# Two-layer decoder step: gained weights of the next layer formed behind a wait on the down products, last factors written in the down stage, two norm factors asked for later

## The chip, the cores and the metric

One core of a Trainium2 chip runs the whole program. The metric is the device time in microseconds (us), the median of the runs. The engines are named as the profile names them: PE (matmul), PEld (the loading of PE's weights), DVE (vector engine), ACT (scalar engine), POOL (GpSimd), SP (which here only issues transfers). A row such as `L246` is line 246 of the kernel before.

## The reference

Two layers run over 1024 prompt tokens and 8 decode tokens, width 1024, MLP width 4096. The parts that matter here are the MLP, which ends each layer, and the two projections that begin layer 1: the shared keys and values (`w_kv`, behind the gain `norm_kv`) and the queries (`w_in_b`, behind the gain `norm_mix_pre[1]`).

```python
def rmsnorm(x, g):
    xf = x.astype(jnp.float32)
    y = xf * lax.rsqrt(jnp.mean(xf * xf, axis=-1, keepdims=True) + EPS)
    return (y * g.astype(jnp.float32)).astype(x.dtype)

def squared_relu_mlp(h, w_up, w_down):
    return jnp.square(jax.nn.relu(h @ w_up)) @ w_down

for l in range(DEPTH):
    if l == N_A_LAYERS:
        ks, vs = jnp.split(rmsnorm(x, norm_kv) @ w_kv, 2, axis=-1)
    h = rmsnorm(x, norm_mix_pre[l])
    ...
    q, qm = split_cols(h @ w_in_b[bl], IN_B_SIZES)
    ...
    f = squared_relu_mlp(rmsnorm(x, norm_ffn_pre[l]), w_ffn_up[l], w_ffn_down[l])
    x = x + rmsnorm(f, norm_ffn_post[l])
```

## The kernel before

All matrices are float32. Each operand of a large matmul is cut into a high and a low part (`split`, L156 to L158: a cast on ACT, a subtraction on DVE), and each product is three matmuls (high by high, high by low, low by high).

**The MLP** (`mlp`) is the same code for both layers, with `l` the layer. Its **up stage** first does 4 of the 32 row tiles of `w_up` plainly (`up_plain`; the squared results go to the buffer `apd` in device memory), and then the other 28 as 14 pairs. A pair is one 2x2 block product done with seven products instead of eight: `wino_weights` (L660 to L675) makes the seven weight combinations on DVE from two loaded tiles `ws`, `product` (L838) runs a product, and `evict` (L640 to L653) adds each PSUM bank into the four results `c11` to `c22` on DVE, whose tile is named `aw` (`am` for the three combinations that `factors` makes). A pair is 168 matmuls of 258 columns. Its results go to the buffer `awd` in device memory. The four plain tiles need four such combinations too: `plain_factors` (L869) loads them from `apd` into tiles `c`, combines them on DVE (L878), and writes them to `awd` (L879). It is a generator: one step is taken at the fourth product of a pair from the sixth pair on.

The **down stage** is a loop of 64 phases (L1127). Phase `t` belongs to one of seven products and does 48 matmuls; the last 16 phases are half as wide. `load_w` fetches a weight block `wr` five phases ahead, `load_a` a factor block `ra` three phases ahead into two buffers (`rap`), `prep` (L984) cuts both two phases ahead, and `phase` (L1033) issues the matmuls; where a product ends, `gather` adds eight PSUM banks into `acc` on DVE. `kept["mm"]` is the name of the last matmul of the phase.

**The folds.** In layer 0 the loop also calls `fold` (L240) twelve times, once for each of the twelve weight tiles of layer 1's first projections. A fold is two halves, and each half is: POOL issues a load of 256 KB into a tile `t` (tag `t3`, two buffers), POOL multiplies it by the gain (128x512, L246), POOL issues the store to the buffer `wfd` in device memory (L247). SP loads from `wfd` at the end of the down stage and after it (L220). The table `folds` gives the phase that calls each fold: 2 to 6, 25 to 29, 36 and 38. A fold's load is placed behind `kept["mm"]` by a dependency of the kind `NOSYNC`.

**What sets the order.** A scheduler puts each engine's instructions in one list when the program is built; an engine runs its list strictly in order. A `NOSYNC` dependency orders two instructions for this scheduler alone and makes no engine wait at run time. A `SYNC` dependency puts a semaphore wait into the instruction. So before the change a fold's load waits only for its tile to be free.

**The norm factors.** `Closing` handles one of four pieces of the MLP's output (pa, pb, pc, pd). `feed` sums squares, `factor` turns them into the norm factor by a matmul with a matrix of ones (L204: `sf<-rb` for pc, `sx<-rf` for pd), two ACT and three DVE instructions. Its second argument says behind how many matmul columns the scheduler puts that matmul; `unit` is 9216 columns.

Of the kernel before, what the change touches and what calls it, by code (L numbers as in the profile page):

```python
# [8 lines left out]
F32 = mybir.dt.float32  # L9
# [7 lines left out]
P = 128  # L17
# [21 lines left out]
ORDER = (1, 7, 6, 5, 2, 3, 4)  # L39
# [10 lines left out]
def hybrid_decoder_step(ctx: ExitStack, tc: tile.TileContext, A, O):  # L50
# [14 lines left out]
    rp = ctx.enter_context(tc.tile_pool(name="rstd", bufs=1))  # L65
# [26 lines left out]
    def nm(s):  # L92
        uid[0] += 1
        return f"{s}_{uid[0]}"
# [2 lines left out]
    turn = [0, 0]  # L97
    xsp = [None]
    late = []
    NOSYNC = mybir.DependencyInfo(mybir.DependencyClass.NoSync, mybir.DependencyReason.DATA)  # L100

    class Row:
# [3 lines left out]
        def __call__(self, mm):  # L106
            if self.prev is not None:
                tc.add_manual_dep(mm.ins, self.prev, NOSYNC, reason="row of tiles")
            self.prev = mm.ins.name
# [16 lines left out]
    def tick(mm, cols):  # L126
        for it in list(late):
            it[1] -= cols
            if it[1] <= 0:
                late.remove(it)  # L130
                tc.add_manual_dep(it[0], mm.ins.name, NOSYNC, reason="behind later matmuls")

# [16 lines left out]
    def tmp3(shape):  # L149
        return view(tp.tile([P, 768], F32, tag="t3", name=nm("t3")), shape)  # L150
# [88 lines left out]
    def fold(i, behind):  # L239
        src, g = (A["w_kv"][i], G_KV) if i < 4 else (A["w_in_b"][i - 4], G_MIXPRE + 1)  # L240
        for h in range(2):
            ks = slice(4 * h, 4 * h + 4)
            ws = tmp3([P, 4, P])
            d = nc.gpsimd.dma_start(ws, src[:, ks, :])
            tc.add_manual_dep(d.ins, behind, NOSYNC, reason="behind later matmuls")
            nc.gpsimd.tensor_tensor(ws, ws, gains[:, g, ks].unsqueeze(2).to_broadcast([P, 4, P]), ALU.mult)  # L246
            nc.gpsimd.dma_start(wfd[i][:, ks, :], ws)  # L247

# [366 lines left out]
    class Slots:  # L615
# [3 lines left out]
        def next(self):  # L619
            self.half ^= 1  # L620
            if self.half == 0:
                self.cur = self.slots[self.i % len(self.slots)]
                self.i += 1
            ks = slice(4 * self.half, 4 * self.half + 4)
            return self.cur[0][:, ks, :], self.cur[1][:, ks, :]
# [50 lines left out]
    def mlp(l, X, ff):  # L676
# [192 lines left out]
        def plain_factors():  # L869
            for q in range(2):  # L870
                rows = [tp.tile([P, 768], F32, tag=tag, name=nm("c"))[:, :HALF] for tag in ("t3", "t3", "tq", "tq")]
                for r, (m, h) in zip(rows, ((0, 0), (0, 1), (1, 0), (1, 1))):
                    nc.sync.dma_start(r, apd[l, :, 2 * q + m, h, :])
                c11, c12, c21, c22 = rows
                for f_, r, a, b, op in ((1, c12, c22, c12, ALU.subtract), (4, c11, c12, c11, ALU.add),
                                        (6, c21, c11, c21, ALU.subtract), (5, c22, c22, c11, ALU.subtract)):
                    yield
                    TT(r, a, b, op)  # L878
                    nc.sync.dma_start(awd[l, f_, NJ - 1, :, q, :], r)  # L879

        plain = plain_factors()
        prepare(2)
        next(xsteps.pop(0))
        pend = None
        for t, (j, i) in enumerate(items):
            if i == ORDER[0]:
                if j == 0:
                    tiles = [tp.tile([P, 768], F32, tag=tag, name=nm("c")) for tag in ("t3", "t3", "tq", "tq")]
                    rows = [x[:, :HALF] for x in tiles]
                else:  # L890
                    tiles = [ff.pools[j % 2].tile([P, 4, HALF], F32, tag="f", name=nm("aw"))]
                    rows = [tiles[0][:, q] for q in range(4)]
            if xsteps:
                next(xsteps.pop(0))
                if xsteps:
                    next(xsteps.pop(0))
            prepare(t + (3 if j == 0 else 5))
            product(j, i, rows)
            if i == ORDER[0] and pend is not None:
                factors(*pend[2:])  # L900
                store(*pend)
                pend = None
            if i == ORDER[3] and 2 <= j < 5:
                square_mean(j - 2)
            if i == ORDER[3] and j >= 5:
                next(plain, None)
            if i == ORDER[-1]:
                more = w4.tile([P, 3, HALF], F32, tag="w4", name=nm("am"))
                pend = (j, tiles, rows, more)
# [75 lines left out]
        def prep(t):  # L985
            p, jj, s = phases[t]
            i = DOWN[p]
            r1, r2 = reg(1, jj), reg(2, jj) if p else None
            r3 = reg(3, jj) if p > 1 else None
            if i == 7:  # L990
                TT(r1, r1, r2, ALU.subtract)
            if i == 6:
                TT(r1, r3, r1, ALU.subtract)
            if i == 4:
                TT(r2, r2, r3, ALU.add)
            wh, wl = wsl[t % 3] if s is None else lasting(jj)
            if s is None or s == 0 and jj > 3:
                split(wh, wl, {1: r1, 7: r1, 6: r1, 5: r2}.get(i, r3))
            if i == 2:
                TT(r3, r3, r1, ALU.subtract)  # L1000
            raw = raws.pop(t)
            n = raw.shape[-1]
            sa = sas[t % 3]
            split(sa[:, 0, :, :n], sa[:, 1, :, :n], raw)
            ready[t] = (wh, wl, sa)
# [52 lines left out]
        unit = 3 * KT * 384  # L1058
        early, late_ = (acc[11], acc[21]), (acc[12], acc[22])
        rb = rbp.tile([P, SUB], F32, tag="rb", name=nm("rb"))  # L1060
# [8 lines left out]
        pc = piece(late_, slice(0, SUB), "sf", (1, 0, SUB))  # L1069
        pd = piece(late_, slice(SUB, HALF), "sx", (1, SUB, 384 - SUB), (2, 132, 132))  # L1070
# [13 lines left out]
        def hook(v):  # L1084
            if -8 <= v < -4:
                split(*lasting(v + 8), reg(3, v + 8))
            if v == -4:
                pa.feed(0, 1, 2, 3)
            if v == 0:
                rooms((pa, "xh0"), (pc, "xl0"))  # L1090
                pa.factor(rp.tile([P, 384], F32, tag="rf", name=nm("rf")), 0.3 * unit)
            if v == 1:
                pb.feed(0, 1, 2, 3)
                pb.factor(rx, 2 * unit)
            if v == 2:
                pa.close(behind=kept["mm"])
            if v == 4 and not l:
                hl[0] = xtiles(0)
                pa.cut(hl)
            if v == 5:  # L1100
                rooms((pb, "xl2"))
                pb.close(behind=kept["mm"])
            if v == 7:
                pc.feed(2, 3, 0, 1)
                pc.factor(rb, 1.8 * unit)
            if v == 9:
                pc.close((2, 3, 0, 1), behind=kept["mm"])
            if v == 11:
                rooms((pd, "xh2"))
            if v == 10 and not l:  # L1110
                rt[0] = rtile(0)
                pa.measure(0, rt[0], 2.3 * unit, Ring())
            if v == 11 and not l:
                hl[1] = xtiles(1)
                pc.cut(hl)
                hl[2] = xtiles(2)
                pb.cut(hl)
# [5 lines left out]
        with tc.high_priority(100):  # L1123
            prep(0)
            prep(1)
        folds = dict(zip((2, 3, 4, 5, 6, 25, 26, 27, 28, 29, 36, 38), (2, 3, 0, 1, 10, 11, 4, 5, 6, 7, 8, 9)))
        for t in range(N):  # L1127
            for u in ([3, 4, 5] if t == 0 else [t + 5]):
                if u < N:
                    load_w(u)  # L1130
            if t + 3 < N:
                load_a(t + 3)
            if t + 2 < N:
                with urgent(2) if t + 2 >= 6 * NJ else ExitStack():
                    prep(t + 2)
            phase(t)
            if l == 0 and t in folds:
                fold(folds.pop(t), kept["mm"])
            hook(t - 6 * NJ)

        st2.close()
        if l:
            with urgent(2):
                pd.finale()
                pd.factor(rp.tile([P, 384], F32, tag="rf", name=nm("rf"))[:, : pd.n], 0)
            pd.close()
        else:
            xs = pool(st, "right", "xs", 3)
            mq = pool(st, "right", "mq", 2)
            pd.feed(2, 3, 0, 1)  # L1150
            pd.factor(rp.tile([P, 384], F32, tag="rf", name=nm("rf"))[:, : pd.n], 1.3 * unit)
            pd.close((2, 3, 0, 1), xs)
            pd.cut(hl, (2, 3, 0, 1))
            rt[1] = rtile(1)
            pc.measure(1, rt[1], 4 * unit, mq)
            pd.measure(1, rt[1], 5 * unit, mq)
            rt[2] = rtile(2)
            pb.measure(2, rt[2], 9 * unit, mq)
            pd.measure(2, rt[2], 10 * unit, mq)
            res = [(hl[c], rt[c]) for c in range(3)]  # L1160
# [1052 lines left out]
```

## Time and profile before

| what | time |
|---|---|
| median of 3 runs (2213.41 to 2217.82) | 2216.09 us |
| the profiled execution, its own time | 2217.6 us |
| its span, first to last instruction | 2215.8 us |
| mean granted PE clock, share of full speed | 0.992 |
| layer 0: seven-product part of the up stage | 536.4 to 844.4 us |
| layer 0: down stage, first to last matmul | 844.4 to 1175 us |
| layer 1: seven-product part of the up stage | 1586.3 to 1872.6 us |
| layer 1: down stage | 1872.6 to 2201 us |
| POOL, all of it | 111.4 us busy |

In a profile row of the stretches, each engine's busy time stands with its number of instructions in brackets (x), then the granted clock, the mean busy share of the 16 DMA engines, and GB/s. In a timeline row the columns are start, duration, engine, line, operation, and in square brackets how long the engine had stood idle and what ended it. In a row of waits: who waited for whom, microseconds in total, how many times, the longest. In a row of a group: count, then busy us, mean ns of one, and idle time before it.

### The profile page before, as it was taken

How to read it: one execution, taken by the hardware profiler on the slowest of the kernel's cores; microseconds unless marked ns; L12 is line 12 of the kernel's file. 1: busy time of each engine (PE TensorE's matmuls, PEld its weight loads, DVE VectorE, ACT ScalarE, POOL GpSimd, SP SyncE). 2: the span in 40 equal slices, each digit the busy share in tenths (PEclk: the TensorE clock that was granted, in tenths of full speed). 3: DMA queues.
4: the chain of work that ended last, by engine and by line, in shares of the span. 5: the costliest groups of instructions: out<-in, count | busy, mean ns of one | idle time of the engine just before them, and what ended most of it. 6: DMA issues, size and time to landing. Idle time of an engine off the chain costs nothing.

```text
span 2215.8 us, 41850 instructions
## 1 busy us (share of the span) xinstructions
PE 2144.0 (97%) x16918; PEld 2042.9 (92%) x16918; DVE 1505.1 (68%) x2839; ACT 1083.0 (49%) x2191; POOL 111.4 (5%) x170
## 2 busy tenths in 40 slices
PE   8999999999999899999999999899999999999997
PEld 6879999899998899999998878599999999999997
DVE  7546648678877676755787355647888777755667
ACT  6454436467544354333654255556654445433453
POOL 0012000000014300000000000200000000000011
PEclk9999999999999999999999999999999999999999
DMA  5422117442676739434354201414275445724345
GB/s 167 142 75 67 36 51 189 142 148 92 207 229 211 240 123 328 154 121 161 92 154 143 76 20 30 164 63 152 91 225 184 158 157 203 280 95 156 105 132 148
DMA packets 142823, 316.40 MB, mean 143 GB/s; under 512 B 15833, under 2 KB 58897, under 8 KB 142273
## 3 DMA queue, kind: packets, MB, share of 16 engines
q1 hardware_dynamic: 125216, 270.43, 38.2%
q0 software_dynamic: 8368, 30.42, 4.3%
q10 hardware_dynamic: 9040, 12.82, 1.6%
q8 instruction: 134, 2.20, 0.4%
q14 instruction: 65, 0.53, 0.1%
HBM read 220.97 MB, written 93.74 MB: 142 GB/s over the span
## 4 chain that ended last, share of the span: by engine, by line
PE 61%; DVE 16%; DMA 13%; ACT 6%; issue 4%; SPq 0%; ACTq 0%; POOL 0%; DVEq 0%
PE mm L257 13%; DMA ws<-in_w_up 7%; PE mx L257 6%; PE mx L1049 5%; PE mx L1050 5%; PE mx L1051 5%; DVE wl L158 4%; PE mm L1049 2%; PE mm L1050 2%; PE mm L1051 2%; ACT wh L157 1%; DMA ra<-awd 1%; DMA t<-xd 1%; PE mx L818 1%; PE mx L819 1%
## 5 line engine op out<-in xcount | busy, mean ns | idle before, releaser
L157 ACT CAST wh<-ws 128x512 fp32r<-128x512 f32 (+1 forms) x258 | 183.9, 720 | 320.3 <-DVE ws L664 125.0
L818 PE MATMUL mx<-xf,wh 128*128 128x258 f32 x1048 | 299.6, 286 | 10.9 <-DVE aw L647 9.7
L819 PE MATMUL mx<-xf,wh 128*128 128x258 f32 x1048 | 296.4, 283 | 0.0
L820 PE MATMUL mx<-xf,wl 128*128 128x258 f32 x1048 | 296.1, 283 | 0.0
L257 PE MATMUL mm<-xh,wh 128*128 128x384 f32 (+1 forms) x864 | 282.1, 326 | 1.5 <-DVE acc L1031 0.9
L158 DVE TENSOR_TENSOR wl<-ws,wh 128x512 fp32r<-128x512 f32 (+1 forms) x258 | 212.1, 829 | 100.3 <-ACT wh L157 99.9
L257 PE MATMUL mm<-xh,wl 128*128 128x384 f32 (+1 forms) x864 | 278.5, 322 | 0.0
L257 PE MATMUL mm<-xl,wh 128*128 128x384 f32 (+1 forms) x864 | 278.1, 322 | 0.0
L157 ACT CAST wh<-wr 128x1024 fp32r<-128x1024 f32 x102 | 106.9, 1048 | 287.8 <-PE sx L1050 275.5
L158 DVE TENSOR_TENSOR wl<-wr,wh 128x1024 fp32r<-128x1024 f32 x102 | 124.9, 1224 | 180.3 <-ACT wh L157 179.8
L1049 PE MATMUL mx<-sa,wh 128*128 128x258 f32 x840 | 239.7, 285 | 4.3 <-DVE aw L651 1.9
L1050 PE MATMUL mx<-sa,wh 128*128 128x258 f32 x840 | 237.3, 283 | 1.6 <-DVE sa L158 1.6
L1051 PE MATMUL mx<-sa,wl 128*128 128x258 f32 x840 | 237.0, 282 | 0.0
L818 PEld LDWEIGHTS mx<-xf,wh 128*128 128x128 f32 x1048 | 198.4, 189 | 14.6 <-DVE aw L647 12.1
L819 PEld LDWEIGHTS mx<-xf,wh 128*128 128x128 f32 x1048 | 198.7, 190 | 0.4
L820 PEld LDWEIGHTS mx<-xf,wl 128*128 128x128 f32 x1048 | 198.8, 190 | 0.0
L257 PEld LDWEIGHTS mm<-xh,wh 128*128 128x128 f32 x864 | 162.8, 188 | 11.1 <-issue 6.3
L257 PEld LDWEIGHTS mm<-xl,wh 128*128 128x128 f32 x864 | 162.8, 188 | 6.8 <-issue 6.0
L257 PEld LDWEIGHTS mm<-xh,wl 128*128 128x128 f32 x864 | 162.4, 188 | 7.0 <-issue 5.1
L1049 PEld LDWEIGHTS mx<-sa,wh 128*128 128x128 f32 x840 | 160.0, 190 | 6.0 <-DVE aw L651 2.4
L1050 PEld LDWEIGHTS mx<-sa,wh 128*128 128x128 f32 x840 | 159.9, 190 | 2.2 <-DVE sa L158 2.0
L1051 PEld LDWEIGHTS mx<-sa,wl 128*128 128x128 f32 x840 | 159.5, 190 | 0.0
(569 smaller groups left out, 5778.6 us busy)
## 6 DMA issues: line engine op xcount, KB each, us to landing
ra<-awd SPq DMA_DIRECT2D x92, 516.0 KB, 3.7
ws<-in_w_up SPq DMA_DIRECT2D x64, 512.0 KB, 4.7
wr<-in_w_downb SPq DMA_DIRECT2D x64, 512.0 KB, 6.1
awd<-aw SPq DMA_DIRECT2D x26, 1032.0 KB, 7.8
awd<-am SPq DMA_DIRECT2D x28, 774.0 KB, 9.5
ws<-in_w_in_a SPq DMA_DIRECT2D x20, 512.0 KB, 3.8
ws<-in_w_out SPq DMA_DIRECT2D x16, 512.0 KB, 3.5
t<-xd SPq DMA_DIRECT2D x20, 384.0 KB, 3.4
```

Of the source, the lines that this page charges most:

```text
L157: nc.scalar.copy(hi, src)
L158: (eng or nc.vector).tensor_tensor(lo, src, f32(hi), ALU.subtract)
L257: mm = nc.tensor.matmul(ps[:M, :n], w_[:, k, :M], x_[:, k, :], start=(i == 0), stop=(i == 3 * KT - 1))
L818: nc.tensor.matmul(ps, wh(k), xh, start=(k == 0), stop=False)
L819: nc.tensor.matmul(ps, wh(k), xl, start=False, stop=False)
L820: mm = nc.tensor.matmul(ps, wl(k), xh, start=False, stop=(k == n - 1))
L1049: nc.tensor.matmul(ps, wh[:, q, ms], h, start=(jj == 0 and q == 0), stop=False)
L1050: nc.tensor.matmul(ps, wh[:, q, ms], lo, start=False, stop=False)
L1051: mm = nc.tensor.matmul(ps, wl[:, q, ms], h, start=False, stop=end)
```

## The change

There are four edits. (1) A fold's first half waits, by a real semaphore, for the last matmul of the phase that it follows; the second half stands behind it in POOL's list. (2) The twelve folds follow phases 14, 16, and so on to 36. (3) `plain_factors` is stepped in the first 13 phases of the down loop instead of in the up stage, with two more empty steps after its loads. (4) The norm factor of pc stands behind 2.5 units of columns instead of 1.8, that of pd behind 2 instead of 1.3.

```diff
+    SYNC = mybir.DependencyInfo(mybir.DependencyClass.Sync, mybir.DependencyReason.DATA)
@@ fold
             d = nc.gpsimd.dma_start(ws, src[:, ks, :])
-            tc.add_manual_dep(d.ins, behind, NOSYNC, reason="behind later matmuls")
+            if h == 0:
+                tc.add_manual_dep(d.ins, behind, SYNC, reason="behind later matmuls")
             nc.gpsimd.tensor_tensor(ws, ws, gains[:, g, ks].unsqueeze(2).to_broadcast([P, 4, P]), ALU.mult)
             nc.gpsimd.dma_start(wfd[i][:, ks, :], ws)
@@ plain_factors, after the four loads of a half
+                yield
+                yield
@@ up stage
-        plain = plain_factors()
...
-            if i == ORDER[3] and j >= 5:
-                next(plain, None)
@@ hook, at phase 48 + 7
-                pc.factor(rb, 1.8 * unit)
+                pc.factor(rb, 2.5 * unit)
@@ down loop
-        folds = dict(zip((2, 3, 4, 5, 6, 25, 26, 27, 28, 29, 36, 38), (2, 3, 0, 1, 10, 11, 4, 5, 6, 7, 8, 9)))
+        folds = dict(zip(range(14, 38, 2), (2, 3, 0, 1, 10, 11, 4, 5, 6, 7, 8, 9)))
+        plain = plain_factors()
...
+            if t < 13:
+                next(plain, None)
             phase(t)
@@ layer 0, after the loop
-            pd.factor(rp.tile([P, 384], F32, tag="rf", name=nm("rf"))[:, : pd.n], 1.3 * unit)
+            pd.factor(rp.tile([P, 384], F32, tag="rf", name=nm("rf"))[:, : pd.n], 2 * unit)
```

How the built lists change is seen at three places. Rows of the change carry its own line numbers, one to four higher, and other buffer numbers; the names are otherwise the same.

POOL, layer 0, the first fold from its second half on and the start of the second fold, with the semaphores that each row waits for in brackets (DMASW: transfers that POOL issued; Pool: POOL itself; PE: matmuls). Before:

```order
L246 TENSOR_TENSOR t_1431_10943<-t_1431_10943,gains 128x512 [waits DMASW1_49]
L247 DMA wfd<-t_1431_10943 128x512 [waits DMASW3_49,Pool_49]
L244 DMA t_1434_11003<-in_w_kv 128x512 [waits DMASW2_49]
L244 DMA t_1435_11007<-in_w_kv 128x512 [waits DMASW5_49,DMASW3_49]
L246 TENSOR_TENSOR t_1434_11003<-t_1434_11003,gains 128x512 [waits DMASW4_49]
```

With the change:

```order
L248 TENSOR_TENSOR t_1457_11634<-t_1457_11634,gains 128x512 [waits DMASW1_49]
L249 DMA wfd<-t_1457_11634 128x512 [waits DMASW3_49,Pool_49]
L245 DMA t_1470_11768<-in_w_kv 128x512 [waits DMASW2_49,PE_49]
L245 DMA t_1471_11772<-in_w_kv 128x512 [waits DMASW5_49,DMASW3_49]
L248 TENSOR_TENSOR t_1470_11768<-t_1470_11768,gains 128x512 [waits DMASW4_49]
```

POOL's 412 instructions stand in the same sequence; the first load of every fold has gained a wait on PE, and nothing else on POOL has moved.

SP, layer 0, in the middle of the up stage (`ws` are weights of the up stage, `c<-apd` and `awd<-c` the loads and stores of `plain_factors`). Before:

```order
L229 DMA ws_8121<-in_w_up 128x1024
L863 DMA awd<-aw_7760 128x4x516
L229 DMA ws_8123<-in_w_up 128x1024
L867 DMA awd<-am_8020 128x3x516
L873 DMA c_8683<-apd 128x516
L873 DMA c_8684<-apd 128x516
L879 DMA awd<-c_8682 128x516
```

With the change:

```order
L230 DMA ws_8121<-in_w_up 128x1024
L865 DMA awd<-aw_7760 128x4x516
L230 DMA ws_8123<-in_w_up 128x1024
L869 DMA awd<-am_8020 128x3x516
L875 DMA c_10743<-apd 128x516
L875 DMA c_10744<-apd 128x516
L883 DMA awd<-c_10742 128x516
```

The transfers of `plain_factors` stand at the same place among the weight loads as before, in both layers, and so do its combinations on DVE: the scheduler still puts them where their inputs are ready.

PE, layer 0, near the end of the down stage (`mm` and `mx` are PSUM banks of the down products, `sf<-rb` the matmul of pc's norm factor). Before:

```order
L1051 MATMUL mm_14024<-sa_10734,wr_13243 128x258
L204 MATMUL sf_14012<-rb_10741,ones 128x258
L1049 MATMUL mm_14024<-sa_10734,wr_13243 128x258
L1050 MATMUL mm_14024<-sa_10734,wr_13243 128x258
L1051 MATMUL mm_14024<-sa_10734,wr_13243 128x258
```

With the change:

```order
L1050 MATMUL mx_14025<-sa_10702,wr_13243 128x258
L1051 MATMUL mx_14025<-sa_10702,wr_13243 128x258
L1052 MATMUL mx_14025<-sa_10702,wr_13243 128x258
L205 MATMUL sf_14012<-rb_10709,ones 128x258
L1050 MATMUL mx_14026<-sa_10702,wr_13243 128x258
```

The matmul of pc's factor stands 9 matmuls later in layer 0 and 24 later in layer 1. That of pd, in layer 0, stands 7 matmuls earlier among the first matmuls of layer 1 (behind 6 of a bank instead of 13); around these two, some DVE and ACT instructions and a few loads of SP have changed places with their neighbours. Everything else in the five lists is in the order of before.

## The prediction

> **What bounds the kernel now.** I read the page's engine table first, then the stretches of the two up stages, then who waits in them.
>
> ```profile
> PE 2144.0 (97%) x16918; PEld 2042.9 (92%) x16918; DVE 1505.1 (68%) x2839; ACT 1083.0 (49%) x2191; POOL 111.4 (5%) x170
> 536.40:844.40 308.00, 290.57 (x2362) 285.71 (x2360) 229.48 (x449) 141.96 (x255) 54.17 (x72) 0.99 0.62 201
> 1586.30:1872.60 286.30, 284.86 (x2361) 283.16 (x2360) 219.86 (x453) 142.54 (x257) 0.00 (x0) 1.00 0.53 172
> ```
>
> PE is the bound, so time is to be had only where PE is idle or slowed. The last two rows are the same code, the seven-product part of the up stage, in layer 0 and in layer 1, from its first matmul to the first of the down stage. Layer 0 takes 308.0 us, layer 1 286.3, for the same number of matmuls. Both hold `plain_factors` and the sums of squares. What only layer 0 has is POOL: 54.17 us in 72 instructions, the twelve folds (24 halves of three). So layer 1 is the control, and layer 0 is **21.7 us** longer.
>
> ```profile
> 600.00:630.00 30.00, 29.25 (x236) 28.32 (x235) 25.02 (x50) 15.24 (x30) 0.00 (x0) 1.00 0.64 198
> 750.00:780.00 30.00, 25.90 (x199) 25.49 (x200) 20.50 (x42) 10.17 (x18) 10.59 (x14) 0.94 0.72 244
> 780.00:810.00 30.00, 30.00 (x252) 29.99 (x252) 23.95 (x50) 17.57 (x32) 0.00 (x0) 1.00 0.31 99
> 652.00:771.00 119.00, 106.35 (x847) 103.54 (x846) 85.03 (x156) 47.58 (x85) 53.10 (x71) 0.99 0.70 229
> 1680.00:1800.00 120.00, 119.20 (x989) 118.45 (x988) 90.05 (x188) 57.02 (x103) 0.00 (x0) 1.00 0.47 155
> L246 POOL TENSOR_TENSOR t<-t,gains x24: 1030/1052/1607, 652.1 to 768.7; 128x512 f32<-128x512 f32 x24
> 645.69 0.58 POOL L244 DMA_DIRECT2D t<-in_w_kv  x1 [306.34 <-ACT aw L851]
> ```
>
> The loss starts and stops with the folds: PE does 236 matmuls in the 30 us before them, 199 in their last 30, 252 right after; across them 847 in 119 us, against 989 in 120 us of layer 1. Although the table calls them in the down stage, they run from 645.69 on, when their tile came free: nothing held them.
>
> How they reach PE:
>
> ```profile
> 667.00 1.05 POOL L246 TENSOR_TENSOR t<-t,gains 128x512 f32<-128x512 f32 x1
> 666.86 1.75 DVE L671 TENSOR_TENSOR ws<-ws 128x512 f32<-128x512 f32 x1
> L671 DVE TENSOR_TENSOR ws<-ws 128x512 f32<-128x512 f32 x6 | 4.1, 692 | 0.2
> L664 DVE TENSOR_TENSOR ws<-ws,ws 128x512 f32<-128x512 f32 x5 | 4.1, 830 | 15.5 <-DMA ws<-in_w_up 15.5
> L664 DVE TENSOR_TENSOR ws<-ws,ws 128x512 f32<-128x512 f32 x6 | 4.2, 693 | 13.4 <-DMA ws<-in_w_up 13.4
> L646 DVE TENSOR_TENSOR aw<-mx,aw 128x258 f32<-128x258 f32 x7 | 2.9, 417 | 0.0
> PE mx L818 <- DVE aw L647: 5.9, 3, 2.3
> PE mm L818 <- DVE aw L647: 3.9, 2, 3.5
> PE mm L818 <- DVE aw L644: 1.6, 2, 1.1
> PE mx L818 <- DVE aw L644: 0.6, 1, 0.6
> PE mm L818 <- DVE aw L647: 0.8, 2, 0.5
> ```
>
> The DVE operation beside POOL's product took 1.75 us where the same one takes 0.692 in layer 1: it is longer by the product's 1.05. Also the wait for the pair's weights grew from 13.4/6 = 2.2 us to 15.5/5 = 3.1 each, with the DMA share at 0.70 instead of 0.47. DVE works in order, so the PSUM reads behind come late and PE waits for a bank (the first four of the last five rows; the fifth is all of it in layer 1's stretch).
>
> **The change part by part.** *Edits 1 and 2, the folds.* They remove from layer 0's up stage 24 loads, 24 products and 24 stores. I take the control: 308.0 - 286.3 = **-21.7 us**. The ends: the named waits give back only 5.9 + 3.9 + 1.6 + 0.6 - 0.8 = 11.2 us; more than the control could come only if layer 0 beat layer 1, for which no row speaks.
>
> The same work lands in phases 15 to 37 of the down stage.
>
> ```profile
> 930.00:1060.00 130.00, 130.00 (x1094) 130.00 (x1093) 72.38 (x85) 48.98 (x49) 0.00 (x0) 1.00 0.42 134
> 870.00:900.00 30.00, 30.00 (x255) 30.00 (x254) 28.18 (x25) 12.70 (x18) 0.00 (x0) 1.00 0.87 304
> 954.24 1.22 DVE L158 TENSOR_TENSOR wl<-wr,wh 128x1024 fp32r<-128x1024 f32 x1 [3.33 <-ACT wh L157]
> 959.98 1.23 DVE L158 TENSOR_TENSOR wl<-wr,wh 128x1024 fp32r<-128x1024 f32 x1 [3.38 <-ACT wh L157]
> 1026.39 0.32 SPq L220 DMA_DIRECT2D ws<-wfd  x1
> 1133.26 1.01 SPq L371 DMA_DIRECT2D t<-xd  x2
> 1251.79 0.30 POOL L2054 MEMSET vsh<- 64x256 f32 x1 [481.02 <-PE mm L257]
> ```
>
> A phase is 5.7 us (959.98 - 954.24), and DVE idles 3.3 us in it. A fold every two phases puts two holds of 1.05 us against 6.6 us of idle, and the splits run two phases ahead of their matmuls: that work hides the folds, and I take 0. Without the cover it costs at most what DVE lost in the up stage, 229.48 - 219.86 = 9.6 us. The transfers: the folds raised the share by 0.70 - 0.47 = 0.23; 0.42 + 0.23 = 0.65, below the 0.87 at which PE still ran full (870 to 900).
>
> The new wait is at the head of POOL's list. Behind it stand only the other folds, and then the memset that now comes after 481 us of idle. SP waits for the folds twice. Its first load of `wfd` (1026.39; about 1005 when 21.7 us earlier) needs the fold of phase 14, which ends near 844.4 + 15 x 5.7 = 930 now and 908 then: some 90 us to spare. Its loads into tile `t` (1133.26) need the last fold, of phase 36: 930 + 22 x 5.7 = 1055, and some 10 us for the fold itself (twelve of them ran from 646 to 771), so over 60 us to spare.
>
> POOL's product reads two operands from SBUF, and so does the stretched DVE operation, while the PSUM reads kept 417 ns beside it. The Trainium skill (SBUF — State Buffer, Who interferes with whom) says that a vector instruction with two SBUF inputs and a GpSimd instruction that reads SBUF exclude each other for a whole instruction, whoever starts first. By that rule the 24 products hold the splits of the down stage just as they held the combinations; the trace agrees for the up stage. It is the third rival below.
>
> *Edit 3, `plain_factors`.* In the built lists its loads, combinations and stores have not moved: **0**. That the control holds them too is why they are no part of the 21.7.
>
> *Edit 4, the factors.*
>
> ```profile
> PE sf L204 <- DVE rb L198: 2.1, 1, 2.1
> PE sx L204 <- DVE rf L198: 1.7, 1, 1.7
> 1161.53 0.28 PE L1050 MATMUL mx<-sa,wr 128*128 128x258 f32 x1
> 1162.59 0.29 PE L1050 MATMUL mx<-sa,wr 128*128 128x258 f32 x1
> 2199.56 0.43 DVE L1031 TENSOR_TENSOR acc<-mm,acc 128x258 f32<-128x258 f32 x1 [4.04 <-PE mm L1051]
> ```
>
> In layer 0 PE stood 2.1 us before pc's matmul. It is now 9 matmuls later, and nine take 1162.59 - 1161.53 = 1.06 us, with what feeds `rb` unmoved: **-1.1 us**. pd's moves 7 matmuls of 384 columns *earlier* by the list, while one square sum fewer stands ahead of it on DVE; its wait of 1.7 us may vanish or double. I take 0, with 1.7 either way. In layer 1 pc's matmul comes 24 later, 24 x 0.118 = 2.8 us; DVE idles 4.04 us just behind that chain (2199.56), so the tail does not move: 0.
>
> **Sum.** 0 - 21.7 - 1.1 = -22.8 us against the profiled execution's own 2217.6 (span 2215.8 and 1.8 around it): 2194.8. That execution lies 1.5 above the median 2216.09 of the runs, so the median to expect is 2216.1 - 22.8 = **2193.3 us**, about 1% faster.
>
> **The rivals.** *Only the waits come back.* PE busy at fewer matmuls might be its own slowness, the clock of 0.94 in one stretch for instance. Then 11.2 + 1.1 us: 2203.8. Against it: the clock is 1.00 in the other stretches, and 142 matmuls are missing there.
>
> *The folds do not move,* because POOL's order is the same and the wait is met early. For it: the order. Against it: the wait on PE in each fold's first load. Then only -1.1: 2215.0.
>
> *The holds recur.* The splits are DVE's whole work in the down stage and each reads twice from SBUF, so each product may meet one. If DVE's 9.6 us reach PE: 2193.3 + 9.6 = 2202.9. Against it: 3.3 us of idle in each phase.
>
> *Slower: the `ra` loads come late.*
>
> ```profile
> ra<-awd SPq DMA_DIRECT2D x92, 516.0 KB, 3.7
> DMA to landing us min/median/max: 10.3/10.9/12.1
> ```
>
> The factor block has two buffers, so a load has about two phases, 11.4 us, to land; it takes 3.7. The second row is the `am` stores of 774 KB beside the folds in the up stage, the slowest transfers there. If the folds drove `ra` past 11.4 us, PE would stop in every phase: at 13 us, 1.6 x 23 phases = 37 us, 2193.3 + 37 = 2230. It decides from 11.4 us on and has eaten the whole gain at 12.4 (1.0 x 23 = 23 us). Against it: three times the present landing, and the stretch with 0.87.
>
> **How the numbers follow.** The sum as worked out has 0.78; only the waits 0.08; the holds 0.06; the folds do not move 0.03; `ra` late 0.05. The likeliest case alone spans 2190 (all of both factor waits gone: 21.7 + 2.1 + 1.7 = 25.5 off, 2190.6) to 2199 (1.7 lost at pd and some four holds that reach PE). The range reaches over the second and the fourth case: **2190 to 2205**. A measurement of this kernel tells 0.2%, 4.4 us, from no change: faster 0.78 + 0.08 + 0.06 = 0.92, same 0.03, slower 0.05.
>
> **What would show it.** Right: layer 0's up stage takes 285 to 289 us from its first matmul to the first of the down stage, with no POOL in it, DVE's combinations at 0.69 us and the clock 1.00 throughout; the 24 products lie in the down stage, two by two about 11.4 us apart; PE does 253 to 255 matmuls in each 30 us there; the wait before `sf` shrinks to about 1.0 us; layer 1 is as before within 2 us. Wrong: an up stage of layer 0 still above 295 us without POOL work (then something else than the folds made it long), PE waiting for `sa` or `wl` in phases 15 to 37 (the holds), or for `ra` (the transfers); or stalls in the first 60 us of layer 1's projections, where the order around pd's factor changed.

## The result, and the profile after

| | median, us | runs | profiled execution's span |
|---|---|---|---|
| before | 2214.75 | 4 (2212.37 to 2217.82) | 2215.8 |
| with the change | 2195.75 | 4 (2193.79 to 2197.23) | 2194.4 |

The ratio is 0.9913, 95% interval [0.9896, 0.993]: 0.9% faster. The forecast was 2193.3 us, 2190 to 2205. By the medians the change gains 19.0 us, by the two profiled executions 21.4, where 22.8 was forecast. The median of before is of four runs, the three that the prediction knew (2216.09) and one more.

The stretches of the two up stages after, in the columns of the prediction, and then the 60 us of each layer in which `plain_factors` runs, both 60 us behind the start of their stage:

```profile
536.80:828.00 291.20, 285.94 (x2362) 283.40 (x2360) 219.01 (x449) 141.81 (x255) 0.00 (x0) 1.00 0.53 170
1566.00:1852.20 286.20, 284.81 (x2362) 283.13 (x2360) 219.77 (x453) 142.55 (x257) 0.00 (x0) 1.00 0.53 172
596.80:656.80 60.00, 57.45 (x465) 56.04 (x464) 47.35 (x97) 28.86 (x55) 0.00 (x0) 1.00 0.64 201
1626.00:1686.00 60.00, 59.88 (x491) 59.03 (x490) 47.17 (x98) 27.92 (x53) 0.00 (x0) 1.00 0.67 221
```

Layer 0's up stage went from 308.0 to 291.2 us. POOL is gone from it, DVE does the same 449 instructions in 219.01 us instead of 229.48, and the DMA share fell from 0.62 to 0.53. It is now like the control in everything but its length: 291.2 against 286.2. More than half of the rest that is missing lies in the 60 us shown: PE does 465 matmuls there and 491 in layer 1, with the same work of `plain_factors` and a DMA share that is no higher. The 26 matmuls are 26 x 0.118 = 3.1 us of the 5.0. Most of that stretch lies ahead of the folds of before: from 600 to 645.69 us, where their first load stood, PE did 349 matmuls before and does 346 now.

The folds in the down stage, first in POOL's timeline (L245 is a fold's load, L248 its product in the change), then as the group of the 24 products over the stage:

```profile
920.21 1.23 POOL L245 DMA_DIRECT2D t<-in_w_kv  x2 [579.88 <-PE sx L1052]
931.40 1.08 POOL L245 DMA_DIRECT2D t<-in_w_kv  x2 [4.32 <-PE sx L1052]
942.85 1.08 POOL L245 DMA_DIRECT2D t<-in_w_kv  x2 [4.47 <-PE sx L1052]
L248 POOL TENSOR_TENSOR t<-t,gains x24: 1037/1055/1757, 923.2 to 1051.8; 128x512 f32<-128x512 f32 x24
```

POOL idles 579.88 us and is released by a matmul of the phase; the next folds start 11.2 and 11.45 us later, two phases each, with the same release.

Did the work that moved there cost PE anything? Two rows of stretches, of the changed kernel and of the kernel before at the same distance from the start of the down stage (the difference of the two starts, 844.4 - 828.0 = 16.4 us), and two of DVE's timeline of the change (L159 is the subtraction of a split):

```profile
900.00:1080.00 180.00, 180.00 (x1513) 180.00 (x1513) 116.46 (x128) 77.52 (x91) 54.96 (x72) 1.00 0.59 192
990.00:1020.00 30.00, 30.00 (x254) 30.00 (x253) 19.41 (x22) 10.23 (x11) 12.59 (x16) 1.00 0.85 276
926.39 1.23 DVE L159 TENSOR_TENSOR wl<-wr,wh 128x1024 fp32r<-128x1024 f32 x1 [0.53 <-ACT wh L158]
1007.56 2.07 DVE L159 TENSOR_TENSOR sa<-ra,sa 128x1032 fp32r<-128x1032 f32 x1
```

```profile
916.40:1096.40 180.00, 180.00 (x1514) 180.00 (x1513) 109.66 (x128) 77.63 (x91) 0.00 (x0) 1.00 0.39 122
```

PE did 1513 matmuls in 180 us, before 1514. DVE did its 128 instructions in 116.46 us instead of 109.66: it was held for 6.8 us in all, in splits and weight combinations of which single ones took 2.07 us instead of 1.23. So the holds do recur in the down stage. The Trainium skill (SBUF — State Buffer, Who interferes with whom) says that a vector instruction with two SBUF inputs contends with a GpSimd instruction that reads SBUF; the trace agrees with it here too. PE lost nothing by the holds, and in the stretch with a DMA share of 0.85 it was busy for all of the 30 us.

The waits of PE around the end of the down stage, after, for pc (`sf`) and pd (`sx`):

```profile
PE sx L205 <- DVE rf L199: 2.3, 1, 2.3
PE sf L205 <- DVE rb L199: 0.7, 1, 0.7
```

By stages, from a stage's first weight load to the next one's (the stretch in the middle is the layer change and layer 1's mixer). In brackets stands what a granted clock below full speed accounts for, (1 - granted clock) x length summed over stretches of 15 us:

| profiled run | up, layer 0 | down, layer 0 | middle | up, layer 1 | from layer 1's down stage to the end |
|---|---|---|---|---|---|
| before | 308.0 (1.6) | 330.1 (3.4) | 411.8 (5.1) | 286.3 (0) | 343.2 (3.4) |
| with the change | 291.2 (0) | 328.7 (3.4) | 409.3 (3.4) | 286.2 (0) | 342.2 (1.6) |

What lies ahead of the table took 536.4 (0) and 536.8 us (1.6). So 16.8 of the 21.4 us come from layer 0's up stage, 1.4 from its down stage, 2.5 from the middle, 0.1 and 1.0 from layer 1, and 0.4 are lost at the start.

### The profile page after: what moved, and what is told of

The parts are those of the page before. It is cut to its first block, busy times and chain, and to the rows that moved or that the text cites. A ratio compares the mean times of both kernels' runs of the same rounds, so it can differ in the third digit from the quotient of the medians.

```text
span 2194.4 us, 41861 instructions
## 1 busy us (share of the span) xinstructions
PE 2137.5 (97%) x16918; PEld 2040.5 (93%) x16918; DVE 1502.1 (68%) x2839; ACT 1083.3 (49%) x2191; POOL 112.4 (5%) x170
## 4 chain that ended last, share of the span: by engine, by line
PE 70%; DVE 11%; DMA 11%; ACT 5%; issue 3%; SPq 0%; DVEq 0%; ACTq 0%
PE mm L259 16%; PE mx L259 8%; DMA ws<-in_w_up 5%; PE mx L1050 5%; PE mx L1051 5%; PE mx L1052 5%; DVE wl L159 3%; PE mm L1050 2%; PE mm L1051 2%; PE mm L1052 2%; PE mx L820 2%; PE mx L821 2%; PE mx L822 2%; DMA ra<-awd 1%; ACT wh L158 1%
## 5 line engine op out<-in xcount | busy, mean ns | idle before, releaser
L159 DVE TENSOR_TENSOR wl<-ws,wh 128x512 fp32r<-128x512 f32 (+1 forms) x258 | 208.6, 816 | 100.6 <-ACT wh L158 100.3
L159 DVE TENSOR_TENSOR wl<-wr,wh 128x1024 fp32r<-128x1024 f32 x102 | 125.4, 1229 | 171.0 <-ACT wh L158 170.6
L159 DVE TENSOR_TENSOR sa<-ra,sa 128x1032 fp32r<-128x1032 f32 (+1 forms) x128 | 144.2, 1126 | 27.1 <-ACT sa L158 26.6
```

Of the source, the lines that this page charges most:

```text
L159: (eng or nc.vector).tensor_tensor(lo, src, f32(hi), ALU.subtract)
```

## The experiments

They were made in three groups, each on one chip with its own runs of the kernel before: 2208.96 us (median of 20 runs) in the first group, 2207.33 (11) in the second, 2210.81 (11) in the third. Ratios go by the group's own runs. Stage lengths are from the one profiled run of each kernel; the kernel before was profiled only for the table above.

| kernel | median, us | ratio to before | up, layer 0 | up, layer 1 |
|---|---|---|---|---|
| folds only | 2195.11 | 0.9923 [0.99, 0.9947] | 290.4 | 285.9 |
| no wait | 2208.17 | 0.9999 [0.9988, 1.0011] | 306.1 | 283.8 |
| transfers only | 2201.82 | 0.996 [0.9942, 0.9977] | 298.4 | 284.8 |
| products only | 2205.56 | 0.9984 [0.9971, 0.9997] | 299.6 | 285.0 |
| the change, second group | 2192.66 | 0.9916 [0.9894, 0.9937] | 290.7 | 284.9 |
| folds only, second group | 2195.62 | 0.9937 [0.9916, 0.9957] | 287.7 | 284.0 |
| factors wait too, second group | 2188.6 | 0.9908 [0.9888, 0.9929] | 286.5 | 283.4 |
| the change, third group | 2194.27 | 0.9931 [0.9915, 0.9946] | 289.9 | 284.7 |
| factors wait too, third group | 2186.51 | 0.9892 [0.9874, 0.9911] | 283.3 | 283.3 |

**Folds only: edits 1 and 2 without 3 and 4.**

```diff
@@ the kernel before, with the change's
+    SYNC = mybir.DependencyInfo(...)
-            tc.add_manual_dep(d.ins, behind, NOSYNC, ...)
+            if h == 0:
+                tc.add_manual_dep(d.ins, behind, SYNC, ...)
-        folds = dict(zip((2, 3, 4, 5, 6, 25, 26, 27, 28, 29, 36, 38), ...))
+        folds = dict(zip(range(14, 38, 2), ...))
```

> The kernel before with edits 1 and 2 alone: the folds wait and follow phases 14 to 36; plain_factors and the two norm factors as before. Theory (the folds are the whole gain but for about 1 us): layer 0's up stage, from its first seven-product matmul to the first of the down stage, 291 us as with the whole change, span 2195 to 2197, ratio to the kernel before about 0.992; waits before sf and sx 2.1 and 1.7 us as before. Rival (the factors carry a good part): span 2200 or more.

It gains 0.8%, as much as the whole change within the intervals, and its up stage of 290.4 us is the change's 291.2. The folds carry the gain. Two details were expected otherwise: the profiled span was 2199.5 us instead of 2195 to 2197 (that run was the longest of four, 2189.49 to 2201.28), and the waits before `sf` and `sx` were 2.2 and 2.8 us instead of 2.1 and 1.7.

**No wait: the change with its first loads back at the scheduler's kind of dependency.**

```diff
-            if h == 0:
-                tc.add_manual_dep(d.ins, behind, SYNC, ...)
+            tc.add_manual_dep(d.ins, behind, NOSYNC, ...)
```

> The changed kernel with the folds' dependency NOSYNC again; table of phases, plain_factors and factors as changed. Theory (only the real wait moves the folds): POOL's products run in the up stage from about 645 us on, that stage takes 305 to 308 us, span 2212 to 2215, ratio 0.998 to 1.0. Rival (the table or the edits 3 and 4 carry the gain): up stage 291 us, span 2195.

With the new table, edit 3 and edit 4 but no wait at run time, the time is that of before (0.9999), and POOL is back in the up stage:

```profile
534.60:840.70 306.10, 289.30 (x2362) 285.38 (x2360) 228.71 (x449) 142.15 (x255) 55.29 (x72) 0.99 0.62 203
```

DVE is at 228.71 us again and the stage at 306.1. Without the semaphore the other edits move no fold, and together they are worth nothing that can be measured. The semaphore with the old table of phases was not run, so what the new table adds to it is open.

**Which half of a fold costs.** The kernel before without the products (the next layer's weights go through without their gains), and the kernel before with the products on the gains alone and with transfers of 64 bytes a partition (layer 1's weights are then read without gains).

```diff
@@ transfers only
-            nc.gpsimd.tensor_tensor(ws, ws, gains[...]..., ALU.mult)
@@ products only
-            d = nc.gpsimd.dma_start(ws, src[:, ks, :])
+            d = nc.gpsimd.dma_start(ws[:, :1, :16], src[:, 4 * h : 4 * h + 1, :16])
...
-            nc.gpsimd.tensor_tensor(ws, ws, gains[...]..., ALU.mult)
-            nc.gpsimd.dma_start(wfd[i][:, ks, :], ws)
+            gk = gains[:, g, ks].unsqueeze(2).to_broadcast([P, 4, P])
+            nc.gpsimd.tensor_tensor(ws, gk, gk, ALU.mult)
+            nc.gpsimd.dma_start(wfd[i][:, 4 * h : 4 * h + 1, :16], ws[:, :1, :16])
@@ products only, layer 1's first loads: w_kv and w_in_b in the place of wfd
```

> The kernel before with the folds' products left out: loads and stores stay in the up stage, the gains are not applied (the next layer's weights are then the plain ones). If POOL's holds on DVE make the up stage long: 291 to 294 us, span 2197 to 2201. If the transfers do: 305 to 308 us, span 2213. If each does half, as I think likely: about 299 us, span 2206.

> The kernel before with the folds' products kept (the same size, the gains with themselves) and their transfers cut to 64 bytes per partition, so that the pace stays; the next layer's weights are read without gains. If POOL's holds on DVE make the up stage long: 305 to 308 us, span 2213. If the transfers do: 290 to 292 us, span 2198, though single DVE operations still take 1.7 us. If each does half: about 299 us, span 2206.

The up stage of each, then two groups of DVE's weight combinations in it (the first one stands right behind the loading of a pair's weights), for transfers only, products only and, without folds, the change:

```profile
536.10:834.50 298.40, 288.28 (x2362) 285.09 (x2360) 218.84 (x449) 141.72 (x255) 26.11 (x48) 0.99 0.63 208
L663 DVE TENSOR_TENSOR ws<-ws,ws 128x512 f32<-128x512 f32 x13 | 9.0, 691 | 29.1 <-DMA ws<-in_w_up 29.1
L670 DVE TENSOR_TENSOR ws<-ws 128x512 f32<-128x512 f32 x14 | 9.7, 690 | 0.3
```

```profile
536.10:835.70 299.60, 288.81 (x2361) 285.25 (x2359) 228.31 (x449) 141.80 (x255) 55.77 (x72) 0.99 0.52 166
L665 DVE TENSOR_TENSOR ws<-ws,ws 128x512 f32<-128x512 f32 x13 | 9.4, 722 | 24.9 <-DMA ws<-in_w_up 24.8
L672 DVE TENSOR_TENSOR ws<-ws 128x512 f32<-128x512 f32 x14 | 11.1, 792 | 0.3
```

```profile
L666 DVE TENSOR_TENSOR ws<-ws,ws 128x512 f32<-128x512 f32 x13 | 9.0, 692 | 24.7 <-DMA ws<-in_w_up 24.6
L673 DVE TENSOR_TENSOR ws<-ws 128x512 f32<-128x512 f32 x14 | 9.7, 690 | 0.3
```

The two halves act through different doors. With the transfers alone DVE's instructions keep their length (691 and 690 ns; 218.84 us in all, against 219.01 without folds), the DMA share is 0.63, and DVE stands 29.1 us in all before the weights of the pairs, against 24.7 without folds. With the products alone the share is 0.52, that wait is 24.9 us, and DVE's instructions are longer (792 ns in the second group shown; 228.31 us in all). Over the changed kernel's 291.2 us the transfers alone cost 298.4 - 291.2 = 7.2 us and the products alone 8.4, both far outside the 287.7 to 291.2 us that the runs of the change and of folds only took. Whether the halves add up isn't shown. Their 15.6 us stand against the 16.8 of the kernel before, but the lowered clock accounts for 1.6 us in each of these three stages; without it 5.6 + 6.8 = 12.4 stand against 15.2. By the medians, over folds only of the same group, they are 6.7 and 10.5, against 13.9 for both. Single runs spread by more than these differences.

**The change and the folds alone, on one chip.**

> The changed kernel again, so that the next two are compared with it on one chip. Theory (the factors gain about a microsecond on PE, the folds the rest): ratio to the kernel before 0.991 to 0.992, layer 0's up stage 290 to 292 us. Rival (the 5 us by which that stage missed the control are a matter of the single profiled execution): a stage of 286 to 288 us this time.

> The folds' wait and table alone (edits 1 and 2), for the second time, now in the same call as the whole change. Theory: 1 to 2 us longer than the whole change, which is the factors' part, and no more than the measurement can tell; the wait before the matmul of sf near 2.1 us again. Rival (the factors carry the 2.5 us by which the middle between the layers became shorter): 3 to 5 us longer than the whole change, with the middle at 411 to 412 us.

The medians differ by 2195.62 - 2192.66 = 3.0 us, with intervals that overlap. The profiled runs show where such a difference can come from. The middle took 407.8 us in this run of the change, in which the clock stayed at 1.00 there, and 412.0 in the folds-only run, where the lowered clock accounts for 5.1. So the sign that was named for edit 4 (folds only: middle at 411 to 412) came out, but edit 4 isn't the reason. Without what the clock accounts for, the middle took 405.9, 407.8 and 404.8 us in the three profiled runs of the change; with the factors as before it took 406.7 before, 406.7 and 406.9 with the folds alone, 404.0 in "transfers only" and 406.4 in "products only".

The waits before pc's and pd's matmuls together were 0.7 + 2.3 = 3.0, 3.9 and 4.2 us in the three profiled runs of the change, 5.0 and 5.2 with the folds alone, and 3.8 before. By these few runs the later factors save about 1.4 us beside the folds (5.1 - 3.7), and nothing against the kernel before.

The 5 us that layer 0's up stage is short of the control were not a matter of one execution: 290.7 and 289.9 us in the other two runs of the change.

**Factors wait too: the change, with `plain_factors` held as the folds are.**

```diff
-                    nc.sync.dma_start(r, apd[l, :, 2 * q + m, h, :])
+                    d = nc.sync.dma_start(r, apd[l, :, 2 * q + m, h, :])
+                    tc.add_manual_dep(d.ins, kept["mm"], SYNC, reason="behind the down matmuls")
...
-            if t < 13:
+            if 1 <= t < 14:
                 next(plain, None)
```

> The change, and the loads of plain_factors wait for the down products too, so that its transfers, combinations and stores leave the up stage in both layers. Theory A (they make the 5 us by which layer 0's up stage missed the control, since they stand in its first part): layer 0's up stage 286 to 288 us, layer 1's 283 to 285, the time 3 to 7 us below the changed kernel. Theory B (the 5 us come from something else in the stage): layer 0's up stage stays at 290 to 292 us and the time within 2 us of the changed kernel. Theory C (its loads now stand among the ra loads of phases 4 to 13 and wait for a tile there): PE waits for ra, the down stage grows by 5 us or more in each layer, slower than the changed kernel by 5 to 20 us.

The loads of `plain_factors` now do leave the up stage. Its up stages were 286.5 and 283.4 us, as theory A had them, and the median was 4.1 us below the change, with overlapping intervals. So the pair was run again.

> The changed kernel a third time, beside the next one. Its layer 0 up stage took 291.2 and 290.7 us, layer 1's 286.2 and 284.9; if these spread by as much as 3 us (as the same code did in the kernel with the folds alone, 290.4 and 287.7), 288 to 291 and 284 to 286 us. Ratio to the kernel before 0.990 to 0.993.

> The kernel whose plain_factors waits too, a second time; its first gave stages of 286.5 and 283.4 us, a median 4 us below the changed kernel and an interval that overlaps with it. Theory (the loads, combinations and stores of plain_factors cost layer 0's up stage some 3.5 us and layer 1's 1.5): 285 to 288 and 282 to 284.5 us again, median 3 to 6 us below the changed kernel of this call. Rival (the differences were spread between executions): stages of 288 to 291 and 284 to 286 us, medians within 2 us.

This time both of its up stages took 283.3 us, the median was 2194.27 - 2186.51 = 7.8 us below the change, more than was expected, and the intervals of the two ratios to before, [0.9874, 0.9911] and [0.9915, 0.9946], do not meet. In this group it is faster than the change and than the kernel before. The rows of this run: the two up stages, 60 us at the place where `plain_factors` used to be, and the first 60 us of the down stage, where it is now; then that place in the change of the same group.

```profile
537.80:821.10 283.30, 283.30 (x2360) 282.70 (x2359) 215.43 (x441) 142.21 (x255) 0.00 (x0) 1.00 0.49 160
1562.90:1846.20 283.30, 283.30 (x2360) 282.70 (x2359) 217.93 (x444) 144.11 (x257) 0.00 (x0) 1.00 0.48 161
597.00:657.00 60.00, 60.00 (x495) 59.40 (x494) 43.84 (x91) 27.22 (x51) 0.00 (x0) 1.00 0.46 151
840.00:900.00 60.00, 60.00 (x506) 60.00 (x506) 47.37 (x45) 23.98 (x29) 0.00 (x0) 1.00 0.85 292
```

```profile
594.00:654.00 60.00, 58.16 (x471) 56.74 (x470) 46.84 (x96) 28.28 (x53) 0.00 (x0) 1.00 0.64 205
```

PE is busy for the whole of both up stages in this run, 283.30 of 283.30 us, and no idle time is left there. At the old place it does 495 matmuls where the change does 471, with the DMA share at 0.46 instead of 0.64; and in the down stage, at a share of 0.85, it is never idle. Theory C, `ra` loads that come late, did not happen: they landed in 3.6 us (median; longest 8.7), in the change in 3.5 (8.2).

## Why the prediction was right, step by step

- *The bound, and layer 1 as the control.* Right in its mechanism. The folds did leave the up stage, POOL and all, and "folds only" and "no wait" show that this is the gain.
- *The term of -21.7 us.* It was too large by 5: the stage gained 16.8 and took 291.2 us, where the prediction's sign was 285 to 289. The step that failed is "Both hold `plain_factors` and the sums of squares", and with it "That the control holds them too is why they are no part of the 21.7". The same work need not cost the same in both layers. The profile of before could have shown it: from 596.4 us to 645.69, ahead of the folds, PE did 379 matmuls, and 395 at the same distance from the start of layer 1's stage, with the DMA share at 0.64 in both. These 16 matmuls (1.9 us) the folds can't have cost. With `plain_factors` taken out the two stages took 283.3 and 283.3 us in one run, 286.5 and 283.4 in the other. By the means of the profiled runs (the change: 290.6 and 285.3; factors wait too: 284.9 and 283.35) it costs layer 0 about 5.7 us and layer 1 about 1.9, which is 3.8 of the 5.3 us by which the layers still differ. That is an estimate, as two runs of one kernel differ by 3.2. Why layer 0 pays more for the same loads and stores was not found; the rows of the stretches show that the DMA share doesn't tell it. Of the 16.8 us gained, 1.6 are the clock's: it fell in this stage in each of the four profiled runs that had folds' work there (1.6 to 1.8 us), and in none of the seven without, so this drop goes with that work. Why is not shown.
- *The mechanism, "How they reach PE".* Right: products that hold DVE's two-input operations, and transfers that delay the weights, each enough by itself to make the stage longer (by 8.4 and 7.2 us). The prediction named both and priced neither.
- *0 for the folds in the down stage.* Right. The holds came, 6.8 us on DVE of the 9.6 allowed, and PE did as many matmuls. The cover named, DVE's idle time in each phase, fits this: nothing of the third rival's price reached PE.
- *0 for edit 3.* Right: nothing moved. What it would have brought is shown by the kernel that makes those loads wait.
- *pc -1.1, pd 0 with 1.7 either way.* pc's wait was 0.7, 2.0 and 1.8 us in three runs, before 2.1; pd's 2.3, 1.9 and 2.4, before 1.7. Their sum is no shorter than before in a way that these runs could tell; the size given was within the spread.
- *The sum.* By the medians 19.0 us came of the 22.8 forecast. The measured median is nearer to the forecast than that (2195.75 against 2193.3) because the median of before came out 1.3 us lower too. Between the profiled executions it is 21.4: 16.8 in the up stage, and 4.6 elsewhere, where 1.1 was forecast. Of these 4.6 the clock, which was lowered for less of the time, accounts for 1.9 (by the brackets, outside this stage, 11.9 us before and 10.0 after), and the rest has no cause that was found. In the second and third group the whole gain was 14.7 and 16.5 us, no more than the 16.8 of the up stage alone. So the nearness is in part luck: a largest term that was 5 us too large, and 3.5 us from elsewhere that were no part of the reasoning.
- *Only the waits come back* (2203.8) fell: PE's listed waits in the stage went from 17.2 to 5.1 us, 12.1 less, but the stage became 16.8 shorter. The other rivals fell too: the waits of the folds are met in the down stage, no hold reached PE, and the loads of `ra` are on time.

## What to carry to other kernels

An order that a scheduler keeps is not an order on the chip. Here the folds, called in a stage that began at 844.4 us, ran from 645.69 on, when their buffer came free; with a wait on a real event they ran where the other engines have room. So look first at where the work ran, and then for the stage in which the engine that sets the pace runs full with idle time beneath it. A control stage prices the sum of all that differs; the same work in both stages cancels only if it costs the same in both. Compare the two stages stretch by stretch where they should be alike, and take one thing out of both to see what it costs.

## What was not expected of the hardware

- Either half of POOL's work disturbs the up stage by itself: the products make it 8.4 us longer, with held DVE operations, and the transfers 7.2, with later weights.
- In the down stage the hold works in both directions: a product that began beside a DVE operation of 1.22 us took up to 1.757 us itself, against 1.055 in the median.
- The DMA share by itself does not tell what PE loses. At 0.85 over 60 us of the down stage it lost nothing. In the up stage it did 24 matmuls fewer at 0.64 than at 0.46, and in layer 1, at 0.67, it did 26 more than in layer 0 at 0.64.
- The granted clock fell at different places from run to run (in the middle it was 0.86 over 30 us before, and 1.00 throughout in one run of the change) and accounts for 6.8 to 13.6 us of a profiled span (summed as in the table by stages). Of two single profiles of this kernel a difference of some 5 us can be the clock alone.
